# Eight first keys of a product-key layer computed densely instead of gathered, and a first layer put in another order

## The chip, the cores and the metric

The kernel runs on one core of a Trainium2 chip. Its engines work beside one another, each through its own queue in order: TensorE (PE, with its weight loads as PEld), VectorE (DVE), ScalarE (ACT), GpSimd (POOL), and SyncE (SP), which here only issues transfers. The metric is the device time of one execution in microseconds, the median over executions.

## The reference, cut to what matters

A model of 256 tokens and width 1024 in float32: `first_block` has two layers (sliding-window attention beside an S5 state space model, then stick-breaking attention, each with a feed-forward layer), and `second_block` has one (mLSTM beside dilated attention, then PEER). The change concerns the S5 part of the first layer and PEER, the last part of all:

```python
def peer(h, w_query, sub_keys1, sub_keys2, expert_u, expert_v):
    # T = 256 tokens, 8 heads, 128 keys in each of two sets, 128*128 experts of 1024
    s1, s2 = scores of the query halves against sub_keys1, sub_keys2
    v1, i1 = top_k(s1, 16); v2, i2 = top_k(s2, 16)
    vc, ic = top_k(v1[..., :, None] + v2[..., None, :], 16)     # per token and head
    e1 = take(i1, ic // 16); e2 = take(i2, ic % 16)
    idx = e1 * 128 + e2                                          # 128 experts per token
    gate = softmax(vc)
    pre = einsum('td,tkd->tk', x, expert_u[idx])
    a = gelu(pre) * gate
    return einsum('tk,tkd->td', a, expert_v[idx])
```

A token thus uses 128 experts: 16 for each of 8 heads. `e1` is the first key and `e2` the second; an expert's row number is `128 * e1 + e2`. The "second product" is the sum over `expert_v`.

## The kernel before

Most of the kernel is float32 matmul with the weights streamed from memory in tiles of 128 x 1024 (512 KB). A `Stream` loads a raw tile through SP (`fetch`), then `load` makes two float32r halves of it, `whi` by an ACT copy and `wlo` by a DVE subtraction (line 73 is the helper of all DVE and POOL products and sums, line 70 of all ACT copies, L67 of other ACT functions). The tiles live in a ring: 4 `raw`, 3 `whi`, 3 `wlo`, and 4 more of 512 KB under the tag `x2`.

**First layer** (to about 112 us). Its input weights are multiplied while DVE builds the tables of the S5 part: `outer` (L627) forms the products of powers of the state's eigenvalues with the input and output matrices, 128 x 1024 each: two tables `bcd` for the input, and two halves of `clr` for the output. `clr` is zero-filled from memory by SP; half of each table's partitions and columns is written. Before, the `clr` halves are made on DVE in temporaries (`oqw`, `oq`: two products and a sum each) and copied by ACT into place. POOL builds the rotations `ec`, `es` of the scan by doubling, in a temporary with the tag `cmG`. Constants come late: the three masks pass through a temporary `ctmp`, which shares the tag `cmG`, and are cast to bfloat16 by DVE (the last is `swab`). `norm_heads` turns the head's square sums into the factors `rq`, `heads` applies them, then scores and softmax follow, in turns with the scan of the S5 part (`states`, `scan_ops`, `carried`). In `even_core` the order on PE, DVE, ACT and POOL is the order in which the code is written (`tc.manual_schedule`). SP has its own order: the zero fill of `clr`, then the write of `uP` to memory (`ud`) and its reading back (`u4`), then further weights.

**PEER.** The first product is dense: `u_step(e)` (L1765), 128 times, one first key at a time, multiplies the 128 expert rows of `expert_u` with first key e by all 256 tokens, in three float32r products that leave two sums; ACT copies one half of the sum to `GS[:, e]`, the DVE adds the other to it one step later (`u_join`). GS is thus [128 second keys, 128 first keys, 256 tokens]. The top-k work of DVE and POOL is cut in pieces with an estimate of their time and fed in by `run_bg(0.85)`, 0.85 us a step, until step 120. `top_e1` leaves, for each of the 128 experts of a token (on the partitions) and the token (a column), the first key `pe1`, the row number `pidx` and the gate `pg`.

The second product works on gathered rows, four tokens a step, in 64 steps `s`; steps 0 to 31 serve the first 128 tokens (accumulators `acc[0]`, two halves of 512 columns), 32 to 63 the others (`acc[1]`):

- `gather` (L1798): four instructions of POOL, each an indirect transfer that fetches the 128 rows (4 KB each) of one token's experts into a slot of 512 KB. There are 14 slots: the ring's ten and four of `x2`. The chain of waits allows eight gathers in flight.
- `spread` (L1809): four bfloat16 matmuls put e2 on all partitions, and DVE compares it with the partition number (`pcol`): a one-hot of the second key, in a tile `o2` (3 buffers).
- `extract` (L1822): four float32 matmuls of that one-hot with `GS[:, :, token]` bring the 128 first keys' values of the right second key; DVE picks the one of `pe1` by comparing with `iota` and summing (L90), then the row norm, the Gelu (ACT) and the gate follow; the four weights stand in `w32`.
- `apply` (L1837): for two halves of 512 columns and four tokens a matmul of `w32` with the gathered slot.

In a step the order is `spread(s+2)`, `extract(s+1)`, `apply(s)`, `gather(s+3)`. `store` (L1846) fetches the residual in two halves `xr` (in the tag of `o2`), adds the accumulator and writes the output; `store(0)` is issued at s = 31, `store(1)` at the end.

## Time and profile before

| what | us |
|---|---|
| median of 3 runs | 1536.12 (1535.79 to 1536.47) |
| the profiled execution's own time | 1537.89 |
| its span, from the first instruction to the last | 1536.2 |
| first layer, to about | 112 |
| `u_step` loop, about | 835 to 1197 |
| gather phase, about | 1197 to 1536 |

The profiled execution is 1.77 us above the median; 1.7 us of its time lie around the span. The page divides the span into 40 slices of 38.4 us and gives each engine's busy share in tenths; the table of windows does so for any stretch, the timeline lists single instructions with the idle time ahead of each in brackets and what ended it, and the waits add up those times by what ended them. Durations of PE are modelled at their ends, so distances between starts are the surer measure there.

### The profile page before, as it was taken

How to read it: one execution, taken by the hardware profiler on the slowest of the kernel's cores; microseconds unless marked ns; L12 is line 12 of the kernel's file. 1: busy time of each engine (PE TensorE's matmuls, PEld its weight loads, DVE VectorE, ACT ScalarE, POOL GpSimd, SP SyncE). 2: the span in 40 equal slices, each digit the busy share in tenths (PEclk: the TensorE clock that was granted, in tenths of full speed). 3: DMA queues.
4: the chain of work that ended last, by engine and by line, in shares of the span. 5: the costliest groups of instructions: out<-in, count | busy, mean ns of one | idle time of the engine just before them, and what ended most of it. 6: DMA issues, size and time to landing. Idle time of an engine off the chain costs nothing.

```text
span 1536.2 us, 23739 instructions
## 1 busy us (share of the span) xinstructions
PE 1474.2 (96%) x8634; PEld 1126.9 (73%) x8634; DVE 1059.9 (69%) x2519; ACT 668.0 (43%) x1248; POOL 391.7 (26%) x516
## 2 busy tenths in 40 slices
PE   6689999999999999999999999999999999999998
PEld 5568788878988888887888888888888544444443
DVE  7887877675566676776569888999555555555554
ACT  5356555565775555647755445444444000000000
POOL 1820100010100000031110002404000777677764
PEclk9889999999999999999999999999999999999999
DMA  8514655554345555453354555555555999999998
GB/s 319 153 37 164 218 190 191 184 176 138 111 137 185 187 191 189 165 187 123 115 187 161 191 184 179 192 181 191 190 182 184 354 409 408 403 408 409 408 391 333
DMA packets 97389, 341.98 MB, mean 223 GB/s; under 512 B 12016, under 2 KB 15220, under 8 KB 96376
## 3 DMA queue, kind: packets, MB, share of 16 engines
q1 hardware_dynamic: 60120, 206.18, 39.2%
q0 software_dynamic: 36864, 134.23, 22.2%
q8 instruction: 68, 1.11, 0.3%
q14 instruction: 49, 0.40, 0.1%
q10 hardware_dynamic: 288, 0.05, 0.0%
HBM read 337.80 MB, written 2.62 MB: 222 GB/s over the span
## 4 chain that ended last, share of the span: by engine, by line
PE 69%; DMA 16%; DVE 6%; issue 4%; POOL 3%; ACT 2%; SPq 0%; POOLq 0%; DVEq 0%; ACTq 0%
PE mm L375 27%; PE mm L376 14%; DMA vt<-in_ev_dram,pidx 12%; PE acc L385 4%; PE acc L386 4%; PE acc L384 4%; PE mm L367 3%; DMA vx<-in_ev_dram,pidx 3%; PE acc L1843 2%; PE acc L247 1%; DVE wlo L73 1%; POOL vt L1804 1%; PE mm L384 1%; PE mm L385 1%; PE mm L386 1%
## 5 line engine op out<-in xcount | busy, mean ns | idle before, releaser
L375 PE MATMUL mm<-x,whi 128*128 128x512 f32 x1808 | 641.8, 399 | 0.0
L73 DVE TENSOR_TENSOR wlo<-raw,whi 128x1024 fp32r<-128x1024 f32 x345 | 434.2, 1260 | 207.6 <-ACT whi L70 194.9
L376 PE MATMUL mm<-x,wlo 128*128 128x256 f32 x1808 | 507.4, 281 | 2.0 <-DVE wlo L73 2.0
L70 ACT ACTIVATE whi<-raw 128x1024 fp32r<-128x1024 f32 x347 | 366.2, 1057 | 186.6 <-issue 92.0
L375 PEld LDWEIGHTS mm<-x,whi 128*128 128x128 f32 x1808 | 340.4, 188 | 82.5
L376 PEld LDWEIGHTS mm<-x,wlo 128*128 128x128 f32 x1808 | 341.8, 189 | 4.5 <-DVE wlo L73 2.8
L1804 POOL DMA_INDIRECT vt<-in_ev_dram,pidx x184 | 172.5, 938 | 187.1 <-DVE wlo L73 117.0
L1843 PE MATMUL acc<-vt,w 128*32 128x512 f32 x736 | 157.9, 603 | 9.0 <-DMA vt<-in_ev_dram,pidx 4.7
L67 ACT ACTIVATE pk<-pk 128x4 f32<-128x4 f32 x64 | 13.2, 205 | 314.2 <-DVE pk L73 314.2
L70 ACT ACTIVATE gs<-mm 128x256 f32<-128x256 f32 x142 | 54.6, 384 | 207.5 <-PE mm L376 207.5
L90 DVE SCALAR_TENSOR_TENSOR jk<-c,pe,mm 128x128 f32<-128x128 f32 x256 | 89.0, 348 | 72.3 <-PE mm L1826 65.4
L1826 PE MATMUL mm<-gs,o 128*128 128x128 f32 x512 | 124.6, 398 | 1.2 <-DVE o L86 1.2
L73 POOL TENSOR_TENSOR nv<-nss 128x2 f32<-128x2 f32 x5 | 1.0, 195 | 434.3 <-ACT nsq L67 434.3
L1826 PEld LDWEIGHTS mm<-gs,o 128*128 128x128 f32 x512 | 98.2, 202 | 6.2 <-issue 2.2
L1843 PEld LDWEIGHTS acc<-vt,w 128*32 128x32 f32 x736 | 27.7, 108 | 97.4 <-DMA vt<-in_ev_dram,pidx 52.6
L86 DVE TENSOR_SCALAR o<-mm,pcol 128x512 f32<-128x512 f32 x64 | 47.9, 750 | 52.0 <-PE mm L1815 52.0
L1843 PE MATMUL acc<-vx,w 128*32 128x512 f32 x288 | 71.6, 603 | 2.9 <-DMA vx<-in_ev_dram,pidx 1.3
L1804 POOL DMA_INDIRECT vx<-in_ev_dram,pidx x72 | 67.6, 938 | 23.4 <-issue 15.5
L385 PE MATMUL acc<-whi,fhl 128*128 128x512 f32 x176 | 69.9, 397 | 1.4 <-DVE fhl L73 1.4
L384 PE MATMUL acc<-whi,fhh 128*128 128x512 f32 x176 | 69.7, 400 | 1.1 <-ACT fhh L70 1.1
L386 PE MATMUL acc<-wlo,fhh 128*128 128x512 f32 x176 | 69.7, 396 | 0.0
L73 DVE TENSOR_TENSOR gs<-gs,mm 128x256 f32<-128x256 f32 x142 | 58.7, 413 | 10.8 <-ACT gs L70 10.7
(520 smaller groups left out, 2014.4 us busy)
## 6 DMA issues: line engine op xcount, KB each, us to landing
raw<-in_w_dram SPq DMA_DIRECT2D x232, 512.0 KB, 4.3
raw<-in_eu_dram SPq DMA_DIRECT2D x128, 512.0 KB, 3.2
vt<-in_ev_dram,pidx POOLq DMA_INDIRECT x184, 9.5
bcd<-in_cst_dram SPq DMA_DIRECT2D x2, 1024.0 KB, 12.5
u<-in_cst_dram SPq DMA_DIRECT2D x1, 2048.0 KB
clr<-in_cst_dram SPq DMA_DIRECT2D x2, 1024.0 KB, 6.2
vx<-in_ev_dram,pidx POOLq DMA_INDIRECT x72, 9.5
x<-in_x_dram SPq DMA_DIRECT2D x2, 512.0 KB, 4.7
```

Source lines behind the costliest of these rows:

```text
L70: return A.activation(o, i, AF.Copy)
L73: return (e or V).tensor_tensor(o, a, b, op=op)
L86: return (e or V).tensor_scalar(o, a, s1, None, op0=op0)
L90: return V.scalar_tensor_tensor(o, a, s, b, op0=op0, op1=op1, **k)
L375: T.matmul(p, hi[:, ks], x2[:, k].rearrange("p a t -> p (a t)"), start=k == 0, stop=False, skip_group_check=True)
L376: T.matmul(p[:, 0:256], lo[:, ks], xh[:, k], start=False, stop=k == 7, skip_group_check=True)
L384: T.matmul(p, xhi, hi, start=first, stop=False)
L385: T.matmul(p, xlo, hi, start=False, stop=False)
L386: T.matmul(p, xhi, lo, start=False, stop=last)
L1804: G.indirect_dma_start(v, None, evr, bass.IndirectOffsetOnAxis(ap=pidx[:, tok(s, g):tok(s, g) + 1], axis=0))
L1826: T.matmul(p[:, g * 128:(g + 1) * 128], o[:, g * 128:(g + 1) * 128], GS[:, :, tok(s, g)], start=g == 0, stop=True, skip_group_check=True)
L1843: T.matmul(acc[j][hf][32 * g:32 * g + 32], w32[:, g], vs[g][:, hf * 512:(hf + 1) * 512], start=i == 0, stop=i == 31, skip_group_check=True)
```

## The change

**The dense keys.** `ND = 8` first keys, 120 to 127, leave the gathers: each gather now carries a bounds check at row 128 * 120 - 1 and is told to leave out rows beyond it without an error; `extract` compares with 120 keys instead of 128, so such experts get the weight 0. What they add to the output is computed for all 256 tokens: `gate_in` and `gate_out` form, for eight tokens a step in steps 0 to 31, the gate of each (second key, dense first key) by a bfloat16 product of one-hots (the gate itself split in three bfloat16 parts `gp`), and multiply it with the Gelu of GS; `dense(i)`, at s = 32, 36, ... 60, multiplies that [128 second keys, 256 tokens] matrix by the 512 KB of `expert_v` for first key 120 + i. `dense_in` splits both into float32r halves and starts the next load. The accumulators are zeroed by four matmuls, since products of two kinds now go into them.

**What goes with it.** GS is stored as [8, 256 tokens, 16], so that the eight dense keys and each token's keys lie together: `u_step`'s copy and add write 64 bytes apart. The gathers have 10 fixed slots (raw 2, whi 2, wlo 2, x2 4), the other four ring tiles serve the dense part. The order in a step is `apply(s)`, `gather(4)`, `spread(s+3)`, `extract(s+2)`, then the gates or the dense product. `o2` has 2 buffers. `store(0)` is issued at s = 60, after `dense(7)`. `spread(0)` and `spread(1)` move into the `u_step` loop.

**The first layer.** The zero fill of `clr` moves behind the reading of `ud`, two weight fetches ahead of its write; `ctmp` takes the tag `qT`; the second `bcd` table waits for a weight split; `clr[:, 0]` is built on DVE inside the heads' code without ACT's copy, `clr[:, 1]` on POOL; the last product of `norm_heads` moves to POOL; the first scan's steps 4 and 5 come after the second softmax.

```diff
-        tmp = sb.tile([128, 4, 512], F32, name="ctmp", tag="cmG")
+        tmp = sb.tile([128, 2, 512], F32, name="ctmp", tag="qT")
...
+        for _ in range(2):
+            W.fetch()
         S.dma_start(ud.rearrange("(m q) t -> q m t", m=4), uP.rearrange("q m t c -> q m (t c)"))
...
+        outer(bcd[0:1], 0, ((pr, bbr, pi, bbi, OP.subtract),), (0,), V)
+        with tc.issue_after(W.los[9].ins):
+            outer(bcd[1:2], 0, ((pr, bbi, pi, bbr, OP.add),), (2,), V)
+        def clr0():
...
+            mul(b_[:, 0], bj(pr), bm(c_re))
+            mul(b_[:, 1], bj(pi), bm(cneg))
+            yield
+            for h in range(2):
+                hs = slice(h * 64, (h + 1) * 64)
+                add(clr[hs, 0, :, :, h, :], b_[hs, 0], b_[hs, 1])
+            yield
...
+        clr1 = lambda: outer([clr[:, 1]], 1, ((pr, cneg, pi, c_re, OP.subtract),), None, G)
...
-        rq3 = norm_heads(rq, ssv, ssq, r, 20, sb, V)
+        rq3 = norm_heads(rq, ssv, ssq, r, 20, sb, V, G)
         taps()
+        clr1()
...
-    GS = p2.tile([128, 128, 256], F32, name="gs")
+    GS = p2.tile([128, 8, 256, 16], F32, name="gs")
...
-        cp(GS[:, e], p[:, 256:512])
-        halves.append((GS[:, e], p))
+        cp(GS[:, e // 16, :, e % 16], p[:, 256:512])
+        halves.append((GS[:, e // 16, :, e % 16], p))
...
+                G.indirect_dma_start(v, None, evr, bass.IndirectOffsetOnAxis(ap=pidx[:, t:t + 1], axis=0), bounds_check=128 * (128 - ND) - 1, oob_is_err=False)
...
-        o = p2.tile([128, 512], F32, name="o2", tag="o2", bufs=3)
+        o = p2.tile([128, 512], F32, name="o2", tag="o2", bufs=2)
...
-            stt(jk, iota, pe1[:, t:t + 1], p[:, g * 128:(g + 1) * 128], OP.is_equal, OP.mult, accum_out=pk[:, g:g + 1])
+            stt(jk[:, 0:128 - ND], iota[:, 0:128 - ND], pe1[:, t:t + 1], p[:, g * 128:g * 128 + 128 - ND], OP.is_equal, OP.mult, accum_out=pk[:, g:g + 1])
...
-            xr = p2.tile([128, 512], F32, name="xr", tag="o2", bufs=3)
+            xr = p2.tile([128, 512], F32, name="xr", tag="o2", bufs=2)
...
+    def gate_in(n, o):
...
+        for i in range(8):
+            act(o[:, i], iota, AF.Abs, bias=pe2n[:, 8 * n + i:8 * n + i + 1])
+        act(o, o, AF.Relu, bias=1.0, scale=-1.0)
+        a = p2.tile([128, 8, 4, ND], BF16, name="ga", tag="cand", bufs=2)
+        tt(a[:, :, 3], iota[:, None, 128 - ND:128].to_broadcast([128, 8, ND]), pe1[:, t8, None].to_broadcast([128, 8, ND]), OP.is_equal)
+        mul(a[:, :, 0:3], a[:, :, 3:4].to_broadcast([128, 8, 3, ND]), gp[:, t8, :, None].to_broadcast([128, 8, 3, ND]))
...
+        act(d, d, AF.Gelu)
...
+    def gate_out(n, o):
...
+        for i in range(8):
+            T.matmul(p[:, i * 3 * ND:(i + 1) * 3 * ND], o[:, i], a[:, i, 0:3].rearrange("p k e -> p (k e)"), start=True, stop=True,
+                     skip_group_check=True)
+        V.tensor_reduce(jk[:, 0:8 * ND], p[:, 0:24 * ND].rearrange("p (t k e) -> p t e k", t=8, k=3), axis=AX.X, op=OP.add)
+        d = GS[:, 7, 8 * n:8 * n + 8, 16 - ND:16]
+        mul(d, d, jk[:, 0:8 * ND].rearrange("p (t e) -> p t e", t=8))
...
+    def dense(i, hi, lo):
...
+                for l, r in ((ah, hi), (al, hi), (ah, lo)):
+                    T.matmul(acc[j][hf], l[:, sl], r[:, c], start=False, stop=False, skip_group_check=True)
...
+        gather(10)
+        S.dma_start(raw_, ev[128 - ND])
+        extract(0)
+        spread(2)
+        extract(1)
+        gate_in(0, o_[:, 0])
         for s in range(NS):
...
+            apply(s)
+            gather(4)
+            if s + 3 < NS:
+                spread(s + 3)
             if s + 2 < NS:
...
+                extract(s + 2)
+            if s < 32:
+                if s < 31:
+                    gate_in(s + 1, o_[:, (s + 1) % 2])
+                gate_out(s, o_[:, s % 2])
+                if s == 31:
+                    dense_in(0, raw_, hi_, lo_)
+            elif s % 4 == 0:
+                i = s // 4 - 8
+                dense(i, hi_, lo_)
+                if i + 1 < ND:
+                    dense_in(i + 1, raw_, hi_, lo_)
+                else:
+                    store(0)
         store(1)
```

**Three places in the order of instructions.** A row is a line of the kernel, the operation, output and inputs by their names, the shape, and a count where rows of one form follow one another; names in brackets are the queues and engines that a row waits for (DMAHW are SP's transfers). The first is SP at the kernel's end, before:

```order
L118 DMA raw<-in_eu_dram 128x1024 [waits DMAHW4_49,DVE_49]
L1850 DMA xr<-xd 128x512 [waits DVE_49,PE_49] x2
L1852 DMA out_dram<-xr 128x512 [waits DVE_49] x2
L1850 DMA xr<-xd 128x512 [waits DMAHW5_49,DVE_49,PE_49]
L1850 DMA xr<-xd 128x512 [waits DMAHW3_49,DMAHW6_49,DVE_49,PE_49]
L1852 DMA out_dram<-xr 128x512 [waits DMAHW7_49,DVE_49]
L1852 DMA out_dram<-xr 128x512 [waits DMAHW0_49,DVE_49]
```

After:

```order
L1921 DMA vraw<-in_ev_dram 128x1024 [waits DMAHW7_49,DMAHW0_49,DVE_49]
L1884 DMA xr<-xd 128x512 [waits DVE_49,PE_49]
L1886 DMA out_dram<-xr 128x512 [waits DVE_49]
L1884 DMA xr<-xd 128x512 [waits DMAHW2_49]
L1884 DMA xr<-xd 128x512 [waits PE_49]
L1886 DMA out_dram<-xr 128x512 [waits DVE_49]
L1884 DMA xr<-xd 128x512 [waits DMAHW5_49]
L1886 DMA out_dram<-xr 128x512 [waits DVE_49]
L1886 DMA out_dram<-xr 128x512 [waits DMAHW0_49,DVE_49]
```

The two loads of `store(0)` stood side by side; now the second stands behind the first half's output and waits for a transfer of SP, and a load of `store(1)` likewise.

The second is DVE at the end, with the multiply-sums of `extract` (L90), its three products and the add of `xr`. Before:

```order
L86 TENSOR_SCALAR o_14506<-mm,pcol 128x512
L90 SCALAR_TENSOR_TENSOR jk,pk<-c_75,pe_8104,mm 128x128 x4
L73 TENSOR_TENSOR pk<-pk,rb_p 128x4
L73 TENSOR_TENSOR pk<-pk,pg 128x4
L73 TENSOR_TENSOR w_14521<-pk,eye 128x128
L90 SCALAR_TENSOR_TENSOR jk,pk<-c_75,pe_8104,mm 128x128 x4
L73 TENSOR_TENSOR pk<-pk,rb_p 128x4
L73 TENSOR_TENSOR pk<-pk,pg 128x4
L73 TENSOR_TENSOR w_14544<-pk,eye 128x128
L73 TENSOR_TENSOR xr<-xr,acc 128x512 x2
```

After:

```order
L73 TENSOR_TENSOR w_15757<-pk,eye 128x128
L86 TENSOR_SCALAR o_15784<-mm,pcol 128x512
L90 SCALAR_TENSOR_TENSOR jk,pk<-c_75,pe_8100,mm 128x120 x4
L73 TENSOR_TENSOR pk<-pk,rb_p 128x4
L73 TENSOR_TENSOR pk<-pk,pg 128x4
L73 TENSOR_TENSOR w_15799<-pk,eye 128x128
L73 TENSOR_TENSOR xr<-xr,acc 128x512 x2
L90 SCALAR_TENSOR_TENSOR jk,pk<-c_75,pe_8100,mm 128x120 x4
L73 TENSOR_TENSOR pk<-pk,rb_p 128x4
L73 TENSOR_TENSOR pk<-pk,pg 128x4
L73 TENSOR_TENSOR w_15848<-pk,eye 128x128
L73 TENSOR_TENSOR xr<-xr,acc 128x512 x2
```

The two adds of `store(0)` stand ahead of the last four multiply-sums now.

The third is the first layer: DVE from the tables `oqw`, `oq` (temporaries of `clr`) and the split `wlo` to the head norm (`ssq`, `ssv`), before:

```order
L73 TENSOR_TENSOR oqw<-pr,ppb 128x1024
L73 TENSOR_TENSOR bcd_95<-oq_719,oq_720 64x64x16 x2
L73 TENSOR_TENSOR oqw<-pi,cneg 128x1024
L73 TENSOR_TENSOR wlo<-raw,whi 128x1024 x2
L73 TENSOR_TENSOR oqw<-oqw 128x1024
L73 TENSOR_TENSOR oq_732<-pr,cneg 128x1024
L73 TENSOR_TENSOR oq_733<-pi,ppb 128x1024
L73 TENSOR_TENSOR oq_732<-oq_732,oq_733 128x1024
L73 TENSOR_TENSOR wlo<-raw,whi 128x1024
L703 TENSOR_REDUCE ssq<-sk__789 128x2
L703 TENSOR_REDUCE ssq<-sk__792 128x2
L73 TENSOR_TENSOR r_819<-nr 128x2
```

After:

```order
L73 TENSOR_TENSOR wlo<-raw,whi 128x1024 x2
L73 TENSOR_TENSOR oq_719<-pr,bbt 128x1024
L73 TENSOR_TENSOR oq_720<-pi,bbt 128x1024
L73 TENSOR_TENSOR bcd_95<-oq_719,oq_720 64x64x16 x2
L73 TENSOR_TENSOR wlo<-raw,whi 128x1024
L715 TENSOR_REDUCE ssq<-sk__775 128x2
L715 TENSOR_REDUCE ssq<-sk__778 128x2
L73 TENSOR_TENSOR r_805<-nr 128x2
L73 TENSOR_TENSOR ssv<-ssq,r_805 128x20
L87 TENSOR_SCALAR ssv<-ssv 128x20
```

And POOL there, after, from the end of its rotations `ec`, `es`:

```order
L73 TENSOR_TENSOR ec<-cmG 128x16x32
L73 TENSOR_TENSOR es<-cmG 128x16x32
L73 TENSOR_TENSOR rq<-rq,nr 128x20
L73 TENSOR_TENSOR cmG<-pr,cneg 128x1024
L73 TENSOR_TENSOR cmG<-pi,ppb 128x1024
L73 TENSOR_TENSOR clr<-cmG 64x64x16 x2
L73 TENSOR_TENSOR sc<-sc,rd 128x8x128
```

The six operations of `clr` are gone from DVE ahead of the norm; `rq` and four operations of `clr` have come to POOL behind the rotations.

## Rows read from the trace of the kernel before

**Rows 1.** The page, 40 slices: busy share of the DMA engines in tenths

```profile
DMA  8514655554345555453354555555555999999998
```

**Rows 2.** Table of windows, gather phase: busy us (instructions) by engine, clock, DMA, GB/s

```profile
core 0: us, PE busy (x) PEld busy (x) DVE busy (x) ACT busy (x) POOL busy (x), PEclk, DMA share, GB/s
1250.00:1300.00 50.00, 48.77 (x276) 21.34 (x275) 27.33 (x120) 2.05 (x10) 36.66 (x40) 1.00 1.03 409
```

**Rows 3.** Timeline of PE, gather phase: start us, duration us, engine, line, operation

```profile
1204.14 0.40 PE L1815 MATMUL mm<-e2b,idb 128*128 128x128 bf16 x4
1204.38 1.94 PE L1826 MATMUL mm<-gs,o 128*128 128x128 f32 x8
1206.25 1.92 PE L1843 MATMUL acc<-vt,w 128*32 128x512 f32 x16
1208.11 0.40 PE L1815 MATMUL mm<-e2b,idb 128*128 128x128 bf16 x4
...
1304.56 0.40 PE L1815 MATMUL mm<-e2b,idb 128*128 128x128 bf16 x4
1309.68 0.40 PE L1815 MATMUL mm<-e2b,idb 128*128 128x128 bf16 x4
```

**Rows 4.** Waits, 1200 to 1537 us: engine, line, released by: us, times, longest

```profile
PEld acc L1843 <- DMA vt<-in_ev_dram,pidx: 52.6, 52, 2.0
```

**Rows 5.** Timeline of POOL, gather phase: early, and steady

```profile
1207.40 0.94 POOL L1804 DMA_INDIRECT vt<-in_ev_dram,pidx  x1 [0.30 <-issue]
...
1302.18 0.94 POOL L1804 DMA_INDIRECT vt<-in_ev_dram,pidx  x1 [0.34 <-issue]
```

**Rows 6.** Groups by line, 960 to 1075 us: count, busy us, mean ns

```profile
L70 ACT ACTIVATE whi<-raw 128x1024 fp32r<-128x1024 f32 x41 | 43.2, 1054 | 0.0
L70 ACT ACTIVATE gs<-mm 128x256 f32<-128x256 f32 x41 | 15.8, 385 | 61.2 <-PE mm L376 61.2
L73 DVE TENSOR_TENSOR gs<-gs,mm 128x256 f32<-128x256 f32 x42 | 17.2, 409 | 0.0
L67 ACT ACTIVATE gs<-gs 128x128 f32<-128x128 f32 x1 | 0.3, 310 | 0.0
```

**Rows 7.** Table of windows, `u_step` loop, columns as in rows 2

```profile
870.00:900.00 30.00, 30.00 (x171) 26.03 (x170) 26.34 (x90) 14.68 (x22) 0.00 (x0) 1.00 0.53 181
960.00:990.00 30.00, 30.00 (x173) 26.06 (x173) 29.79 (x53) 14.25 (x22) 13.66 (x13) 1.00 0.57 193
```

**Rows 8.** The page, DMA issues: count, median us from issue to landing

```profile
vt<-in_ev_dram,pidx POOLq DMA_INDIRECT x184, 9.5
```

**Rows 9.** The tile `xr`, its four loads and four adds

```profile
DMA to landing us min/median/max: 2.0/6.2/6.9
```

**Rows 10.** Timeline, end of the kernel

```profile
1530.16 1.90 PE L1843 MATMUL acc<-vt,w 128*32 128x512 f32 x10 [0.22 <-DMA vt<-in_ev_dram,pidx]
1531.24 0.69 DVE L73 TENSOR_TENSOR xr<-xr,acc 128x512 f32<-128x512 f32 x1 [5.56 <-PE acc L1843]
```

**Rows 11.** Groups by line and shape, 1200 to 1537 us

```profile
L90 DVE SCALAR_TENSOR_TENSOR jk<-c,pe,mm 128x128 f32<-128x128 f32 x256 | 89.0, 348 | 72.3 <-PE mm L1826 65.4
```

**Rows 12.** Groups by line and shape on DVE, 112 to 180 us

```profile
L73 DVE TENSOR_TENSOR os<-yg,sg 128x256 f32<-128x256 f32 x4 | 2.5, 623 | 0.4 <-ACT sg L67 0.4
L73 DVE TENSOR_TENSOR sol<-os,soh 128x256 fp32r<-128x256 f32 x4 | 1.7, 425 | 2.0 <-ACT soh L70 2.0
```

**Rows 13.** Timeline of POOL, first layer

```profile
39.20 2.97 POOL L73 TENSOR_TENSOR cmG<-ec,zr 128x16 f32<-128x16 f32 x1 [10.92 <-DVE swab L188]
...
71.47 1.26 POOL L73 TENSOR_TENSOR es<-cmG 128x512 f32<-128x512 f32 x1
```

**Rows 14.** Timeline of DVE, first layer

```profile
31.70 0.16 DVE L73 TENSOR_TENSOR zr<-t,t 128x16 f32<-128x16 f32 x1
...
63.54 1.33 DVE L73 TENSOR_TENSOR wlo<-raw,whi 128x1024 fp32r<-128x1024 f32 x1 [3.27 <-ACT whi L70]
...
66.24 1.07 DVE L73 TENSOR_TENSOR ssv<-ssq,r 128x20 f32<-128x20 f32 x1
...
74.93 0.69 DVE L73 TENSOR_TENSOR qn<-acc,rq 128x512 f32<-128x512 f32 x1
```

More of the change, by code (lines that the diff above doesn't have):

```diff
@@ L466, in even_layer @@
         mul(kn_g, qn_g, kn_g)
-        for i in range(2):
-            zeros(clr[:, i].rearrange("p s j h q -> p (s j h q)"))
         a_re, a_im = ppa[:, 0:16], ppa[:, 16:32]
@@ L585, in even_layer @@
                                            uds[:, :, 0:256 - 64 * d_])
+        for i in range(2):
+            zeros(clr[:, i].rearrange("p s j h q -> p (s j h q)"))
         b_re, b_im, c_re, c_im = (ppb[:, i * 256:(i + 1) * 256].rearrange("p (s q) -> p s q", s=16) for i in range(4))
@@ L924, in even_core @@
         smax(0, 0)
+        next(clr0)
         scores(1, 0)
@@ L1781, in tile_kernel @@
     NS = 64
+    ND = 8
     slots = []
```

131 lines of the change are left out of this document (77 added, 54 removed).

## The prediction

> **What bounds the kernel now.** I read the page first: of a 1536.2 us span the last eighth is the only stretch in which the DMA digits stand at 9 [rows 1]. That stretch is the end of PEER, the 64 steps in which expert rows are gathered and applied, and the table of windows says what bounds it: from 1250 to 1300 us the DMA engines are busy all the time at 409 GB/s, while DVE works 27 of 50 us [rows 2]. A step gathers 4 x 128 rows of 4 KB, 2.10 MB, which at 409 GB/s takes 5.13 us; PE's steps are 5.12 us apart (1304.56 to 1309.68), while at the phase's start, with gathers in hand, they were 3.97 us apart (1204.14 to 1208.11: 0.24 of `spread`, 1.87 of `extract`, 1.86 of `apply`) [rows 3]. The waits agree: the weight loads of `apply` wait 52.6 us for gathered rows in `vt` slots alone [rows 4]. POOL, which issues the gathers, is close behind: one instruction takes 0.94 us plus 0.30 us of issue where nothing holds it, 1.24 us, and 1.28 us in the steady stretch [rows 5]. Four are 4.97 us. So a step whose DMA work shrinks gains at most 5.12 - 4.97 = 0.15 us, 10 us over 64 steps, before POOL is late instead. That cap decides much below.
>
> Ahead of it, the `u_step` loop (128 steps of some 2.8 us) is bound by PE with DVE just behind it, and the first layer (20 to 112 us) by a chain through DVE, POOL and ACT. The change touches all three.
>
> **Gathers, first half (s < 32).** Of the 32768 gathered rows 2356 name a first key of 120 or more, as I counted from the reference's inputs: 1100 in the first 128 tokens, 1256 in the others. If the bounds check drops them, DMA in this half falls 6.7%, to 4.79 us a step, and POOL's 4.97 us rules. But new work enters the same steps. On ACT `gate_in` adds eight 128x128 Abs (a 128x128 activation takes 310 ns), a Relu of 128x1024 (nearest 1054 ns) [rows 6] and a small Gelu: some 3.8 us. It starts behind the Gelu of `extract`, which comes some 5.0 us after the step's start (1.86 + 0.24 + 1.87 on PE, then 1.0 of DVE: the last multiply-sums and a product). PE's `gate_out`, one step later and 3.97 us into it, waits for it; so the step cannot be under 5.0 + 3.8 - 3.97 = 4.8 to 5.0 us. PE itself has 3.97 plus eight small bfloat16 matmuls (four with 128 columns take 0.24 us at the head of a step, so 0.5 to 0.8 us): it is covered. Three engines within 0.2 us of one another seldom give the largest alone: I take 5.06 us, **-2 us** in 32 steps; bounds -5 (POOL's floor) and +6 (a step of 5.3 us).
>
> **Gathers, second half.** Seven of the eight dense loads of 512 KB start at s = 31 to 52: 3.67 MB at 409 GB/s are +9.0 us of DMA. The dropped rows are 1256 x 4 KB = 5.14 MB, -12.6 us if all sixteen engines lose alike, and nothing if the busiest keeps its rows. No row of before shows which engine takes which row, but the eight heads, whose sixteen rows each lie together in a gather, drop between 2.0% and 12.6%, so an even loss is unlikely. I take a third, -4: **+5 us**. The bounds are -4 (POOL's cap of 0.15 us x 32, whatever DMA saves) and +9 (nothing dropped, or a dropped row that costs a packet). PE has 3.97 + 2.8 / 4 = 4.7 us a step here (a 512-column matmul is 0.23 us by the `u_step` rows: 173 matmuls of mean 384 columns in 30 us, [rows 7]), which DMA covers.
>
> The Trainium skill, page "DMA: Bandwidth & Descriptors", section "The descriptor swizzle", ties a row's engine to its partition in a 128-partition transfer. By that rule my count of the inputs leaves the busiest engine 1995 of its 2048 rows, 2.6%, and the second half's saving is -4.3 us as an estimate, in place of the -12.6 of an even loss. No row of before shows it, and the rule speaks against the change.
>
> `store(0)` leaves s = 31, where its two reads and two writes of 256 KB (1.05 MB) shared the queue: **-2.6 us**. Ten slots in place of fourteen matter little: a gather lands 9.5 us after its issue [rows 8], 7.4 gathers deep, but when the fourth of a step lands only six can be in flight until `apply` has read them. With the zeroing matmuls, `extract(1)` and `gate_in(0)` ahead of the first `apply`, **+2 us** (0 to +4).
>
> **The end.** Here the change adds a wait that I think it pays in full. `xr` and the spread's output share tag `o2`, now with 2 buffers. When `store(0)` is issued at s = 60, one of them holds `spread(63)`, so its second `xr` takes the buffer of the first: in SP's order that load waits for the first output's landing. Both adds stand in DVE ahead of the four multiply-sums of `extract(63)`, so `apply(63)` waits for the store. From the start of `apply(60)`: its matmuls, `spread`, `extract(62)` end at 4.0; the first `xr` lands 6.2 us later [rows 9] at 10.2, with gathers still flowing; add 0.69 [rows 10], the output lands at about 16.5; the second `xr`, now alone, lands 2.0 us later [rows 9] at 18.6; add, four multiply-sums of 0.39 (0.348 [rows 11] and the read of the accumulator), the three small products and the Gelu: `w32(63)` at 22. Without it `apply(63)` starts when the last gather lands, at 15.3. **+7 us**, 5 to 10. What follows it is as before (6.0 us from 1530.16 to the span's end [rows 10]).
>
> **The `u_step` loop.** GS becomes [8, 256, 16]: the ACT copy (385 ns) and the DVE add (409 ns) of each step [rows 6] now step 64 bytes from element to element. The nearest strided row, a DVE product that writes 16 bytes apart, takes 623 ns where its contiguous like takes 425 [rows 12]: +0.2 us on 409, up to +0.4 as both a read and the write are strided. From 960 to 990 us DVE is busy 29.79 of 30 us [rows 7], ten steps with no room; most other stretches leave about 3 us in 30, 0.28 us a step. Twenty steps at 0.1 us: **+2 us**; 0, if DVE's slack takes all, to +8 (0.2 us in forty steps). The new gate splits in `top_e1` are fourteen small operations, taken into this. `extract` reads GS contiguously now, which may shorten its 1.87 us; PE waits for DMA there, so I count nothing.
>
> The Trainium skill, page "SBUF — State Buffer", section on the port swizzle, note on SBUF cachelines, says that accesses that each go to a new 16-byte line pay a penalty. The rows of the 623 ns product agree, and for 64 bytes it would speak for the upper end, +8 us.
>
> **First layer.** Before, POOL's rotation chain waits 10.92 us for the last mask cast (`swab`) until 39.20 and ends at 72.73 [rows 13]; on DVE six operations for `clr`, and on ACT four copies, stand ahead of `whi`, for which DVE waits 3.27 us; then the head norm runs from 66.24 until `qn` starts at 74.93 [rows 14], its first operations on 20 columns at 1.07 us beside POOL. After, the table's work is behind the heads, POOL's buffer no longer waits for `swab` but for the angles that DVE has by 31.86 [rows 14], some 7 us earlier, and the norm's last product is queued on POOL behind the chain, at about 66: the heads start some 8.5 us earlier. But four 128x1024 operations (1.33 us [rows 14]) come back on DVE ahead of the scans, and four on POOL run beside the heads' DVE work and slow it as the 1.07 us operations were slowed. The fetches moved ahead of `ud` find their weights earlier and change no wait on the chain. **-4 us**, -9 to +1.
>
> **Sum.** -2 + 5 - 2.6 + 2 + 7 + 2 - 4 = +7.4 us on the profiled execution's 1537.89 us. That one is 1.8 us above the median of 1536.12, so in medians 1543.5: I say 1543 us.
>
> **Rivals.** *The gathers run at POOL's pace (faster).* Skipped rows thin all engines, every step is near 4.97 to 5.0 us (-9), the store leaves (-2.6), the first layer gives -7, the end costs 5 and `u_step` 1: -12, some 1524 us; with half of the first layer's gain 1529. For it: the 0.04 us by which POOL is throttled, and DMA's busy share of 1.03. Against it: the heads' uneven shares and the dense loads. Chance 0.31.
> *Gains and the end cancel.* The first layer gives -8 and the rest +8: within 0.2%, which is about what a measurement of this kernel can tell from no change, 1536 us. Chance 0.15.
> *The checked gather is slower (slower, another mechanism).* If the bounds check lengthens POOL's instruction, it decides from 0.04 us on, since 1.24 + 0.04 = 1.28 is DMA's pace; at +0.1 us the loss is 256 x 0.06 = 15 us on top of the rest, 1558 us. The same time results if dropped rows still take their packet and the strided writes cost their upper end: +4 and +6 more. Against it: before has no checked gather, so nothing supports a price. Chance 0.16.
> *The forecast*, 1538 to 1550: chance 0.38.
>
> Slower by over 0.2% are the last two, less a little: 0.52; faster 0.32; same 0.16. The range must reach into the faster case and the slower gather: 1525 to 1558.
>
> **What would show it.** Right: gathers of POOL still 0.94 us; fewer bytes on their queue; PE's steps at 5.0 to 5.1 us in the first half and 5.2 to 5.3 in the second; two adds of `xr` on DVE ahead of the last multiply-sums, 7 us apart, with PE idle; the add of `u_step` at 0.6 us or more; heads from about 67 us. Wrong: steps of 5.0 us throughout; an `apply(63)` that starts with its last gather; or a POOL instruction over 1.0 us.

## The result, and the profile after

| | before | after |
|---|---|---|
| median of four runs, us | 1535.95 (1534.87 to 1536.47) | 1556.55 (1553.96 to 1557.53) |
| the profile's span, us | 1536.2 | 1555.7 |

The change makes the kernel slower: the ratio of the times is 1.013, with an interval of 1.0118 to 1.0143, 20.6 us. The forecast was 7 us slower, so the sign was right and the size a third of what came.

From the page of the kernel after: the span; the granted clock, DMA's busy share and its rate in 40 slices (38.9 us each here); and the gathers' queue.

```profile
span 1555.7 us, 25283 instructions
PEclk9889999999999999999999999999999999999998
DMA  8515655543335555543444554555556999999997
GB/s 324 143 42 180 216 189 187 185 165 130 137 115 200 187 190 189 184 151 115 151 176 164 189 185 170 182 183 191 196 184 208 333 375 374 376 386 381 383 362 278
...
q0 software_dynamic: 36864, 124.60, 21.3%
```

The same queue before:

```profile
q0 software_dynamic: 36864, 134.23, 22.2%
```

Against [rows 1] and [rows 2] the last eighth still has 9s for DMA, but the rate has gone from 409 to about 380 GB/s. The queue has moved 124.60 MB where it was 134.23: the rows are indeed left out, some 2355 by the bytes where the prediction counted 2356. It still has 36864 packets. The table of windows shows the same, and which engines have more to do now (ACT 35.76 of 50 us where it had 2.05):

```profile
core 0: us, PE busy (x) PEld busy (x) DVE busy (x) ACT busy (x) POOL busy (x), PEclk, DMA share, GB/s
1250.00:1300.00 50.00, 40.94 (x352) 19.45 (x352) 37.20 (x167) 35.76 (x105) 37.94 (x39) 0.97 1.00 377
1400.00:1450.00 50.00, 47.51 (x299) 21.82 (x299) 29.90 (x117) 6.65 (x15) 36.68 (x36) 1.00 1.01 382
```

Where the time went is read most safely from the starts of single matmuls, at the same places of the program. Before, in order: the last matmul of the `u_step` loop, and the first of `apply(4)`, `apply(32)` and `apply(60)`.

```profile
1195.78 0.28 PE L376 MATMUL mm<-x,wlo 128*128 128x256 f32 x1
...
1218.73 1.06 PE L1843 MATMUL acc<-vt,w 128*32 128x512 f32 x6
...
1364.39 1.18 PE L1843 MATMUL acc<-vt,w 128*32 128x512 f32 x5
...
1512.32 1.06 PE L1843 MATMUL acc<-vt,w 128*32 128x512 f32 x6
```

After:

```profile
1196.90 0.28 PE L376 MATMUL mm<-x,wlo 128*128 128x256 f32 x1
...
1224.38 1.06 PE L1877 MATMUL acc<-vx,w 128*32 128x512 f32 x6
...
1371.42 0.62 PE L1877 MATMUL acc<-vx,w 128*32 128x512 f32 x2
...
1523.85 1.05 PE L1877 MATMUL acc<-vraw,w 128*32 128x512 f32 x4
```

| stretch | before, us | after, us | difference |
|---|---|---|---|
| to the last matmul of the `u_step` loop | 1195.8 | 1196.9 | +1.1 |
| from there to `apply(4)` | 23.0 | 27.5 | +4.5 |
| `apply(4)` to `apply(32)` | 145.7 | 147.0 | +1.4 |
| `apply(32)` to `apply(60)` | 147.9 | 152.4 | +4.5 |
| `apply(60)` to the end of the span | 23.9 | 31.8 | +7.9 |

The sum is +19.4 of the 19.5 us between the spans. No single stretch holds the loss. These are one profile against one: where two kernels run the same code up to the end of the `u_step` loop, as after and the last but one of the experiments do, two profiles still differ by 1.2 us there.

**POOL.** Two gathers of the steady stretch, to be held against [rows 5]:

```profile
1297.16 0.99 POOL L1836 DMA_INDIRECT vx<-in_ev_dram,pidx  x1 [0.30 <-issue]
1298.45 0.99 POOL L1836 DMA_INDIRECT vx<-in_ev_dram,pidx  x1 [0.30 <-PE mm L1910]
```

An instruction takes 0.99 us where it took 0.94, and the next starts after the same 0.30 us of issue, 1.29 us apart in all. POOL waits for nothing here beyond its issue: the idle time is 0.30 us again, not the 0.34 of the steady row in [rows 5], although DMA's share is still 1.00. From `gather` 16 to 128, the rows of `apply(4)` to `apply(31)`, it takes 146.2 us with 1.0 us of idle time beyond the issue, and those applies take 147.0: in the first half POOL has become the engine that sets the step. Four such gathers are 5.17 us; before, DMA set 5.12.

**The end.** The timeline from the first residual load of `store(0)`:

```profile
1529.01 0.33 SPq L1884 DMA_DIRECT2D xr<-xd  x1
...
1535.54 0.69 DVE L73 TENSOR_TENSOR xr<-xr,acc 128x512 f32<-128x512 f32 x1 [4.05 <-DMA xr<-xd]
1536.26 0.34 SPq L1886 DMA_DIRECT2D out_dram<-xr  x1
...
1542.39 0.80 SPq L1884 DMA_DIRECT2D xr<-xd  x2
1545.12 0.69 DVE L73 TENSOR_TENSOR xr<-xr,acc 128x512 f32<-128x512 f32 x1 [8.89 <-DMA xr<-xd]
...
1547.88 0.29 DVE L73 TENSOR_TENSOR w<-pk,eye 128x128 f32<-128x128 f32 x1
1548.23 1.06 PE L1877 MATMUL acc<-vwhi,w 128*32 128x512 f32 x2 [8.41 <-DVE w L73]
```

It went in the order that the prediction has: first load at 1529.01, add at 1535.54, output, second load only at 1542.39, second add at 1545.12, and behind it on DVE `w32(63)`; PE waited 8.41 us for it. `apply(63)` starts 24.4 us after `apply(60)` (1548.23 - 1523.85).

**The start of the gather phase** (ACT's `gate_in(0)`, PE's `extract(2)`, and the next gather):

```profile
1204.56 2.43 ACT L67 ACTIVATE vraw<-c,pe2n 128x128 bf16<-128x128 f32 x8
...
1207.98 0.24 ACT L67 ACTIVATE gs<-gs 128x64 f32<-128x64 f32 x1
1208.27 1.16 PE L1857 MATMUL mm<-gs,o 128*128 128x128 f32 x8 [3.82 <-ACT gs L67]
...
1213.37 0.98 POOL L1836 DMA_INDIRECT vwlo<-in_ev_dram,pidx  x1 [4.08 <-PE acc L1877]
```

`extract(2)` waits 3.82 us for the Gelu of `gate_in(0)`, which overwrites the dense columns of the tokens 0 to 7 in GS; token 2 is one that `extract(2)` reads. `apply(1)` is late by that, and POOL, with ten slots, stands 4.08 us until it has read them.

**The clock of PE** falls at both places. Windows of the kernel after, and one of before, with the columns as above:

```profile
1204.50:1208.20 3.70, 0.00 (x0) 0.00 (x0) 1.75 (x6) 3.67 (x11) 2.89 (x3) 1.00 0.94 338
1209.80:1213.00 3.20, 3.20 (x16) 0.43 (x8) 2.68 (x16) 1.80 (x7) 0.00 (x0) 0.50 0.91 321
1548.20:1551.00 2.80, 2.77 (x16) 0.59 (x16) 0.69 (x1) 0.00 (x0) 0.00 (x0) 0.50 0.27 94
```

```profile
1200.00:1520.00 320.00, 308.97 (x1730) 139.28 (x1730) 176.01 (x757) 12.94 (x63) 230.41 (x246) 1.00 1.02 404
```

After PE has stood still from 1204.50 to 1208.20, `apply(1)` runs at 0.50, the lower of the clock's two levels (1.2 of 2.4 GHz), and takes 3.5 us to the next matmul (1209.55 to 1213.07), where `apply(2)` takes 1.9. The gather that POOL waits for is released at its end. `apply(63)`, after the wait of 8.41 us, runs at 0.50 too. Before, the clock is 1.00 throughout. So some 1.7 us of the loss at the start, and some 1.3 at the end (the matmuls of `apply(63)` on one slot start 0.86 us apart, those of `apply(2)` 0.44), come from the clock that fell with the wait; this is read from the trace, and no run isolates it.

**The first layer.** DVE from the head's factors to the first scan, after:

```profile
67.30 0.69 DVE L73 TENSOR_TENSOR qn<-acc,rq 128x512 f32<-128x512 f32 x1 [0.33 <-POOL rq L73]
...
76.06 1.22 DVE L73 TENSOR_TENSOR clq<-pr,ppb 128x1024 f32<-128x1024 f32 x1
77.20 1.22 DVE L73 TENSOR_TENSOR clq<-pi,cneg 128x1024 f32<-128x1024 f32 x1
...
79.93 2.45 DVE L73 TENSOR_TENSOR clr<-clq 64x1024 f32<-64x1024 f32 x2
...
83.88 1.22 DVE L872 TENSOR_TENSOR_SCAN g<-rho_t,g 128x512 f32<-128x512 f32 x1
```

And that scan before:

```profile
85.66 1.17 DVE L860 TENSOR_TENSOR_SCAN g<-rho_t,g 128x512 f32<-128x512 f32 x1
```

The heads start at 67.30 instead of 74.93 [rows 14], 7.6 us earlier; the scan at 83.88 instead of 85.66, 1.8 us earlier.

**The `u_step` loop**, ACT's copy and DVE's add of GS from 960 to 1075 us, and a window:

```profile
L70 ACT ACTIVATE gs<-mm 128x256 f32<-128x256 f32 x41 | 25.9, 631 | 55.6 <-PE mm L376 55.6
L73 DVE TENSOR_TENSOR gs<-gs,mm 128x256 f32<-128x256 f32 x41 | 25.5, 621 | 0.0
```

```profile
960.00:990.00 30.00, 29.79 (x169) 25.40 (x168) 29.79 (x50) 15.81 (x22) 13.67 (x13) 1.00 0.50 182
```

The copy has gone from 385 to 631 ns and the add from 409 to 621 ns [rows 6]; PE, which was busy for all 30 us from 960 to 990, has lost 0.21 there [rows 7].

### The profile page after: what moved, and what is told of

Same layout as the page of the kernel before. It is cut to its first block, busy times and chain, and to the rows that moved or that the text cites. A ratio compares the mean times of both kernels' runs of the same rounds, so it can differ in the third digit from the quotient of the medians.

```text
span 1555.7 us, 25283 instructions
## 1 busy us (share of the span) xinstructions
PE 1461.0 (94%) x8989; PEld 1119.9 (72%) x8990; DVE 1132.7 (73%) x2704; ACT 811.0 (52%) x1580; POOL 420.3 (27%) x521
## 3 DMA queue, kind: packets, MB, share of 16 engines
q0 software_dynamic: 36864, 124.60, 21.3%
## 4 chain that ended last, share of the span: by engine, by line
PE 65%; DVE 11%; DMA 10%; issue 5%; POOL 4%; ACT 4%; POOLq 0%; SPq 0%; DVEq 0%; ACTq 0%
PE mm L375 23%; PE mm L376 12%; PE acc L385 4%; PE acc L386 4%; PE acc L384 4%; PE acc L1877 4%; DMA vx<-in_ev_dram,pidx 3%; PE mm L367 3%; DVE wlo L73 3%; DMA vwhi<-in_ev_dram,pidx 2%; DMA vraw<-in_ev_dram,pidx 2%; ACT vraw L67 2%; PE mm L1857 2%; PE acc L247 1%; POOL cmG L73 1%
## 5 line engine op out<-in xcount | busy, mean ns | idle before, releaser
L70 ACT ACTIVATE gs<-mm 128x256 f32<-128x256 f32 x142 | 86.9, 612 | 188.7 <-PE mm L376 188.7
L1836 POOL DMA_INDIRECT vx<-in_ev_dram,pidx x100 | 100.8, 1008 | 33.5 <-issue 19.5
L90 DVE SCALAR_TENSOR_TENSOR jk<-c,pe,mm 128x120 f32<-128x120 f32 x256 | 86.8, 339 | 25.3 <-PE mm L1910 9.2
L1877 PE MATMUL acc<-vx,w 128*32 128x512 f32 x400 | 97.7, 610 | 3.7 <-DMA vx<-in_ev_dram,pidx 3.5
L73 DVE TENSOR_TENSOR gs<-gs,mm 128x256 f32<-128x256 f32 x142 | 85.7, 603 | 10.8 <-ACT gs L70 10.8
L1836 POOL DMA_INDIRECT vraw<-in_ev_dram,pidx x52 | 53.0, 1019 | 129.6 <-DVE wlo L73 110.7
L1857 PE MATMUL mm<-gs,o 128*128 128x128 f32 x512 | 72.8, 283 | 8.2 <-ACT gs L67 7.6
L67 ACT ACTIVATE vraw<-c,pe2n 128x128 bf16<-128x128 f32 x256 | 77.8, 386 | 0.0
L1877 PE MATMUL acc<-vwhi,w 128*32 128x512 f32 x208 | 65.3, 644 | 12.0 <-DVE w L73 8.4
L1857 PEld LDWEIGHTS mm<-gs,o 128*128 128x128 f32 x512 | 62.8, 192 | 10.9 <-ACT gs L67 8.5
```

What stands on the lines that cost most here:

```text
L67: return A.activation(o, i, f, **k)
L70: return A.activation(o, i, AF.Copy)
L73: return (e or V).tensor_tensor(o, a, b, op=op)
L90: return V.scalar_tensor_tensor(o, a, s, b, op0=op0, op1=op1, **k)
L1836: G.indirect_dma_start(v, None, evr, bass.IndirectOffsetOnAxis(ap=pidx[:, t:t + 1], axis=0), bounds_check=128 * (128 - ND) - 1, oob_is_err ...
L1857: T.matmul(p[:, g * 128:(g + 1) * 128], o[:, g * 128:(g + 1) * 128], GS[:, :, tok(s, g)], start=g == 0, stop=True, skip_group_check=True)
```

## The experiments

All kernels but the last two were run on chips where the kernel before takes 1576 to 1582 us, those two (both repairs without the check, and what is worth keeping) on one where it takes 1536 as it does for the result. Each kernel is compared with before on its own chip.

**What the parts cost.** The first layer's part alone (all hunks of the diff ahead of the line 700 of before, and that of `even_core`), expected:

> The kernel before with the first-layer part of the change alone. Theory 1 (the first layer gains little: the two traces are 1.8 us apart from the end of that layer on, where I had forecast 4): 1.8 us faster than before, 1534.2, with every stretch from 120 us on 1.5 to 1.8 us early. Rival (the part gains the 4 us forecast and the rest of the change takes some of it back in the first layer): 1532.

Measured: ratio 0.9987 (0.9973 to 1.0002), 2 us faster by its middle. The interval reaches 1, and it holds the sizes of both theories. The trace speaks for theory 1: its heads start at 67.54 and its first scan at 84.14, 1.5 us earlier than before's.

The kernel before with a bounds check that drops nothing:

```diff
-            G.indirect_dma_start(v, None, evr, bass.IndirectOffsetOnAxis(ap=pidx[:, tok(s, g):tok(s, g) + 1], axis=0))
+            G.indirect_dma_start(v, None, evr, bass.IndirectOffsetOnAxis(ap=pidx[:, tok(s, g):tok(s, g) + 1], axis=0), bounds_check=128 * 128 - 1, oob_is_err=False)
```

> The kernel before with a bounds check on every gather, at the table's last row, so that no row is dropped. Theory 1 (the check itself lengthens POOL's instruction, as it stands at 0.99 us after the change where it was 0.94): gathers 0.99 us, 1.29 us apart instead of 1.28, steps of 5.17 us instead of 5.12, 3 us slower in all, 1539. Rival (the length comes from the dropped rows, or from ACT and DVE beside POOL): gathers 0.94 us, steps 5.12, no change.

Measured: ratio 0.9995 (0.9983 to 1.0007). Its POOL row of the gather phase, from the table of groups:

```profile
L1804 POOL DMA_INDIRECT vt<-in_ev_dram,pidx x175 | 173.7, 992 | 84.2 <-issue 40.5 <-remote 22.8 <-PE mm L1826 10.1
```

The instruction's 992 ns stand against 938 [rows 5: 0.94], with no row dropped and no gate work beside it: the price is the check's own. The time didn't move: on this chip the steps are 5.9 us (165.4 us from `apply(4)` to `apply(32)`), so something else held them, and this run can't tell what the price does where POOL is the bound. A second run of the same kernel, on another chip:

> The kernel before with a bounds check on every gather at the table's last row, so that nothing is dropped. Theory 1: the check alone makes POOL's instruction 0.99 us, gathers 1.29 us apart; where the kernel before has steps of 5.12 us set by DMA, they become 5.17, 3 us slower in all. Rival (no price of its own, or POOL not the later one): no change.

Measured: 1.0005 (0.9994 to 1.0017). The price in POOL's row is shown; what it costs where steps are 5.12 us was not measured by this kernel.

The kernel after without the check (`bounds_check=..., oob_is_err=False` taken out), so that all rows come and the dense keys' rows get the weight 0. It ran on three chips:

> The kernel after without the bounds check: all rows are fetched again, those of the dense keys get the weight 0. Theory 1 (POOL's checked gather at 1.29 us apart sets the steps after the change, so the 9.6 MB that are dropped buy nothing): POOL falls to 1.24, DMA becomes the bound again at 5.13 us a step and 9 us of dense loads: within 4 us of after, 1553 to 1558. Rival (DMA still sets the steps after the change): the 9.6 MB come back at 409 GB/s, 23 us slower than after, 1580.

> The kernel after without the bounds check: all rows are fetched, those of the dense keys get the weight 0. Theory 1 (POOL's checked gather, 1.29 us apart, sets the steps after the change, so that the 9.6 MB dropped buy little): within 4 us of after. Rival (DMA still sets the steps): the 9.6 MB come back at the chip's rate, over 20 us slower than after.

> The kernel after without the bounds check, all rows fetched, those of the dense keys with the weight 0. Theory 1 (POOL sets the steps after the change): within 4 us of after. Rival (DMA sets them): over 20 us slower than after.

Measured: 1.0119 (1.0092 to 1.0146), 1.0125 (1.0100 to 1.0150) and 1.0120 (1.0098 to 1.0142), where the kernel after itself, run on the second of these chips alone, had

> The kernel after, unchanged, beside the next three on one chip. Where gathers move at about 405 GB/s in the kernel before, 20 us slower than before; the yardstick for the three. If memory is slower on the chip and before itself takes longer, both theories expect the gap to before to shrink or hold, since DMA and not POOL then sets the steps of both.

1.0136 (1.0108 to 1.0163). Dropping 9.63 MB, 23.5 us of transfer at 409 GB/s, buys nothing that these runs can see, so the rival, 20 us slower, doesn't hold on these chips. It doesn't follow that POOL sets the steps there: they are some 5.9 to 6.0 us, well above POOL's 5.17 with the check and 4.97 without, and the runs with half the bytes below show that on such chips neither bound holds them.

**The waits at the end and at the start.** `store(0)` in the raw tile of the dense part, free by then:

```diff
-    def store(j):
+    def store(j, into=None):
...
-            xr = p2.tile([128, 512], F32, name="xr", tag="o2", bufs=2)
+            xr = into[:, c] if into is not None else p2.tile([128, 512], F32, name="xr", tag="o2", bufs=2)
...
-                    store(0)
+                    store(0, raw_)
```

> The kernel after with the two residual halves of store(0) in the free raw tile of the dense part, so that neither load waits for an output or for the spread's buffer. Theory 1 (the wait at the end costs 7 us, as forecast): apply(63) starts with its last gather, 6 to 8 us faster than after, 1549. Rival (the last gathers, which POOL issues late, set the end anyway): 0 to 2 us faster, 1555.

> The kernel after with the two residual halves of store(0) in the dense part's free raw tile, so that no load waits for an output or for the spread's buffer. Theory 1: apply(63) starts with its last gather, 6 to 8 us faster than after. Rival (the last gathers set the end): 0 to 2 us faster.

Measured: 1.0101 (1.0065 to 1.0138) and 1.0128 (1.0095 to 1.0162), against 1.0136 for after on the second chip (it was not run on the first): faster in both, but within the intervals, and with steps that differ between two profiles of the same chip by more than this. The timelines decide the mechanism. After, on the second chip, with its two adds and `apply(63)`:

```profile
1583.99 0.69 DVE L73 TENSOR_TENSOR xr<-xr,acc 128x512 f32<-128x512 f32 x1 [3.73 <-DMA xr<-xd]
...
1591.45 0.69 DVE L73 TENSOR_TENSOR xr<-xr,acc 128x512 f32<-128x512 f32 x1 [6.78 <-DMA xr<-xd]
...
1594.56 0.13 PEld L1877 LDWEIGHTS acc<-vwhi,w 128*32 128x32 f32 x2 [11.91 <-DVE w L73]
```

And with the repair, where both adds stand together and the next thing that PE waits for is a gather:

```profile
1584.37 1.28 DVE L73 TENSOR_TENSOR vraw<-vraw,acc 128x512 f32<-128x512 f32 x2
...
1588.58 0.14 PEld L1877 LDWEIGHTS acc<-vraw,w 128*32 128x32 f32 x2 [0.85 <-DMA vraw<-in_ev_dram,pidx]
```

From `apply(60)` to the end of the span the two profiles have 33.8 and 23.5 us. So the wait is the one named, and it goes. The medians alone leave its size open.

The groups of `gate_in` in another order, tokens 128 to 255 first:

```diff
+    GO = list(range(16, 32)) + [4 * b + a for a in range(4) for b in range(4)]
...
-        t8 = slice(8 * n, 8 * n + 8)
+        m_ = GO[n]
+        t8 = slice(8 * m_, 8 * m_ + 8)
```

> The kernel after with the groups of eight tokens that gate_in takes in turn put in another order (tokens 128 to 255 first), so that no product of extract reads columns of GS that a Gelu has just overwritten. Theory 1 (the 3.8 us wait of extract(2) for gate_in(0) at the phase's start, which holds POOL back by 4.1 us, and four shorter ones cost what they show): 4 to 6 us faster than after. Rival (POOL catches up, or ACT's gate work of some 4 us a step holds PE just as long one matmul later): 0 to 1 us.

Measured: 1.0188 (1.0146 to 1.0230), no faster, rather slower. `extract(2)` no longer waits, but `gate_out(0)` behind it waits 4.52 us for ACT instead, and POOL still stands 4.09 us at that place. Both repairs together:

> The kernel after with both repairs: the residual halves of store(0) in the dense part's free raw tile, and gate_in's groups of eight tokens in the order that keeps its Gelu away from what extract reads. Theory 1 (start and end cost 4 and 7 us, the rest is POOL at 1.29 us a gather): 10 us faster than after, still 10 us slower than before, with POOL idle for nothing but its issue from the first apply on. Rival (the gate work or the dense loads hold the steps, and both repairs only move the wait): under 5 us faster than after.

Measured: 1.0090 (1.0069 to 1.0111), 7 us less than the 1.0136 that after had on another chip, with intervals that just touch; between the two theories.

**Without the dense work.** `gate_in`, `gate_out`, `dense_in`, `dense` and the first dense load taken out; the dense keys are missing from the output:

> The kernel after without gate_in, gate_out, the dense loads and the dense products; what the eight dense keys add to the output is left out. Theory 1 (POOL's checked gather is the floor of a step): steps of 5.17 us in both halves, the start without its 4 us wait, the end's wait of 7 us as it was: 10 us faster than after. Rival (the rows dropped let DMA go faster than before once the dense work is away): steps of 4.8 to 5.0 us, 20 us faster than after or more.

Measured: 1.0061 (1.0044 to 1.0078), 12 us less than after had on another chip. It is still slower than before, although it has 7% fewer bytes in the gather phase and none of the dense work. The rest of the change is left in it: the check, the ten slots, the wait at the end, the stride of GS and the first layer. The theory's 10 us were met, its steps of 5.17 us not: they are 5.9 us on this chip.

**Half the bytes.** On those chips DMA moves about 360 GB/s in the gather phase, and to take DMA out of the way the gathers fetch 2 KB a row, from another place of the table:

```diff
-            G.indirect_dma_start(v, None, evr, ...
+            G.indirect_dma_start(v[:, 0:512], None, evh, ...
...
-                T.matmul(acc[j][hf][32 * g:32 * g + 32], w32[:, g], vs[g][:, hf * 512:(hf + 1) * 512],
+                T.matmul(acc[j][hf][32 * g:32 * g + 32], w32[:, g], vs[g][:, 0:512],
```

> The kernel before with gathers of 2 KB instead of 4 KB a row (from another place of the table, the product on the first half for both halves; the output is another): DMA has 2.6 us of work in a step. Both theories: POOL's unchecked gathers, 1.24 us apart, set steps of 4.97 us, some 16 us faster than before. This is POOL's floor without the check.

> The same with a bounds check that drops nothing. Theory 1 (the check alone costs POOL 0.05 us an instruction): gathers 1.29 us apart, steps of 5.17 us, 12 us slower than without it. Rival (POOL's wider spacing after the change came from something else): as without it.

> The kernel after with gathers of 2 KB, the products on the first half. Theory 1 (POOL's checked gather is the floor of the steps after the change): 5.17 us a step in both halves, hardly faster than after, with the start's and the end's waits as they were. Rival A (the gate work on ACT, DVE and PE sets the first half): first half at 5.24 us or more as after, second half shorter. Rival B (DMA sets the steps after): both halves go to 5.0 us or less, 20 us faster.

> The same without the check: DMA and POOL's check are both out of the way. Theory 1: steps of 4.97 us in both halves, 12 us faster than with it. Rival A (gate work): the first half stays at 5.1 us or more. This tells what the gate work would allow had the check been free.

Measured: 1.0004 (0.9987 to 1.0021), 0.9988 (0.9972 to 1.0003), 1.0103 (1.0057 to 1.0150) and 1.0107 (1.0078 to 1.0136). The gains that the theories put on half the bytes failed: they change nothing. The check changes nothing either, as its rival has it, though not for the rival's reason: POOL's instruction is 1.00 us with it and 0.95 without here too. The windows of the first:

```profile
1250.00:1300.00 50.00, 40.21 (x250) 20.37 (x240) 21.72 (x95) 1.64 (x8) 32.15 (x34) 0.83 0.63 180
1259.00:1264.00 5.00, 2.56 (x13) 0.59 (x16) 4.14 (x22) 0.41 (x2) 3.79 (x4) 0.50 0.49 129
1267.00:1272.00 5.00, 5.00 (x38) 2.42 (x40) 2.05 (x11) 0.20 (x1) 3.78 (x5) 1.00 0.70 205
```

DMA is busy 63% of the time and moves 180 GB/s, POOL is busy 32 of 50 us; neither holds the steps, which are 6.0 us. The granted clock of PE is 0.83 here, where it was 1.00 in the gather phase of [rows 2]: it goes between its two levels, as from 1259 to 1264 us (0.50) and from 1267 to 1272 (1.00), again and again in this phase on that chip. Why it does so there and not on the other is open. So these runs say nothing on POOL's floor; they say that on such a chip the gather phase isn't bound by what the change saves either.

**Both repairs and no check**, on a chip like that of the result:

> The kernel after with both repairs (start and end) and without the bounds check, all rows fetched. Theory 1 (the dropped bytes buy nothing, since POOL with the check is no faster than DMA without it): as g_fix within 4 us, some 10 us faster than after. Rival (DMA sets the steps after the change): 20 us slower than g_fix.

Measured: 1554.04 us, ratio 1.0117 (1.0100 to 1.0133), against 1.0130 for after: 2 us faster than after, not the 10 expected, and nowhere near the 20 us slower of the rival. Two windows and two lines of its start:

```profile
1250.00:1300.00 50.00, 45.32 (x354) 19.84 (x346) 37.19 (x162) 36.65 (x107) 36.04 (x39) 1.00 1.03 408
1400.00:1450.00 50.00, 47.43 (x294) 20.64 (x293) 29.50 (x114) 6.58 (x15) 33.20 (x36) 1.00 1.02 408
```

```profile
1206.89 0.39 PE L1912 MATMUL mm<-ga,vraw 128*128 128x24 bf16 x8 [2.73 <-ACT vraw L67]
...
1210.66 0.94 POOL L1836 DMA_INDIRECT vwlo<-in_ev_dram,pidx  x1 [2.86 <-PE acc L1877]
```

With POOL's unchecked 0.94 us, DMA is back at 408 GB/s and 1.02 to 1.03 of its time: it sets the steps again, with all rows and the dense loads. By the stretches of the table above (one profile against one, spans 1551.4 and 1555.7): to the loop's end -1.2, to `apply(4)` -1.5, 28 steps of the first half +1.8 (148.8 us), 28 of the second +1.7 (154.1), from `apply(60)` to the end -5.0 (26.8). So dropping the rows, check and all, is worth 3.5 us of the 23.5 that their bytes take, by the starts of the applies; by the starts of the 224 gathers that serve these steps it is 1.5 us (301.7 and 300.2). Both are as small as the difference of two profiles, and the kernel with both repairs and the check was not run on this chip. The end is shorter by 5 us, and the start by 1.5: `extract(2)` doesn't wait any more, but `gate_out(0)`, the next on PE, waits 2.73 us for the same ACT work, `apply(1)` again runs at the clock's lower level (0.50 from 1206.6 to 1209.6), and POOL still stands 2.86 us. The wait that only moves is the rival that I had set against that repair.

**What is worth keeping.** The kernel before with the first layer's part, and `store(0)` behind the last gather:

```diff
-            if s == 31:
+            if s == 62:
                 store(0)
```

and `o2`, `xr` with 4 buffers.

> The kernel before with the first-layer part of the change, and store(0) issued after the last gather (s = 62) with 4 buffers of the tag o2, so that its 1 MB no longer shares the queue with the gathers. Theory 1 (first layer 1.8 us, store(0) 2.6 us at s = 31 of which 1 us comes back at the end): 3 us faster than before. Rival (the store's transfers cost the same wherever they lie, the first layer's gain is lost by the gather phase): no change.

Measured: 1533.58 us against 1536.25, ratio 0.9982 (0.9972 to 0.9992): faster than before by the 3 us expected, and so than after. The two steps beside the old place of `store(0)` take 10.2 us (1354.27 to 1364.51 for `apply(31)` to `apply(33)`) where they took 11.6. The prediction put 2.6 us on the store.

## Why the prediction was right in sign and wrong in size

| term | forecast, us | measured, us |
|---|---|---|
| first layer | -4 | -1.6 at the start of the `u_step` loop |
| `u_step` loop | +2 | +2.0 by 1111 us, +0.7 more at its end |
| start and slots | +2 | +4.5 |
| gathers, first half | -2 | +1.4 |
| gathers, second half, with `store(0)` gone | +5 - 2.6 | +4.5 |
| end | +7 | +7.9 |

**Right.** The end: mechanism and place, and the size within 1 us. Part of the last is luck: the second add, put 18.6 us after `apply(60)`, started 21.3 us after, and `apply(63)`, put at 22, at 24.4; but the last gather that `apply(63)` needs before, put at 15.3, came at 17.8, so that the errors cancel. What follows was to be as before, 6.0 us, and took 7.4 at the lower clock. The `u_step` loop: +0.2 us on each of the two operations, and +2.0 us where DVE has no slack. The rows are dropped, and `extract` is faster (its matmuls 283 ns where they were 398), which the prediction counted as nothing.

**The step that failed most: POOL's floor.** The prediction took 4.97 us for four gathers as the cap on what a step can gain. With the check it is 5.17, above the 5.12 that DMA needed before. It had named this as a rival, with the right point from which it decides ("from 0.04 us on"), gave it 0.16 and no price, since before has no checked gather. The check costs 0.054 us, just over that point. From then on no dropped row can shorten a step, so the -2 of the first half and the -4 of saved rows in the second were not to be had; the first half came 3.4 us above its term, and +1.4 is 28 steps of the 0.05 us between 5.17 and 5.12. The price need only exceed 0.04. It explains the lost gains, not the whole error: of the 12 us by which the stretches came out above their terms, the gathers hold 5.5, the start 2.5, the first layer 2.4, the end and the `u_step` loop 1.6.

The groups of the gather phase show ACT's Abs of `gate_in` after the change:

```profile
L67 ACT ACTIVATE vraw<-c,pe2n 128x128 bf16<-128x128 f32 x256 | 77.8, 386 | 0.0
```

**The second half** has a floor of 28 x 5.17 = 144.8 us by POOL and took 152.4. Two of POOL's rows there tell where the rest lies:

```profile
1373.81 2.00 POOL L1836 DMA_INDIRECT vx<-in_ev_dram,pidx  x1 [0.30 <-PE acc L1877]
...
1404.09 0.99 POOL L1836 DMA_INDIRECT vx<-in_ev_dram,pidx  x1 [1.69 <-PE acc L1877]
```

A dense product stands between two applies on PE, so the slots of the next come free late and POOL stands (1.69 us at 1404.09); and three gathers that begin beside DVE's 1.23 us split of the dense tile take 1.9 to 2.0 us instead of 0.99. In all, POOL's 112 gathers for these steps take 154.0 us, with 6.1 us of idle time beyond the issue and 3.3 us of longer instructions. An engine that sets the pace can't make such time up. The prediction had put the dense loads on DMA alone and spread the dense product evenly over four steps of PE, where DMA would cover it. That these waits make up the 7.6 us above the floor is read from the trace, and no run isolates it. One idle stretch of 1.80 us, before the gather at 1487.26, has no releaser in the trace.

**The start** was put at +2 for the work ahead of the first `apply`, and that cost nothing: `apply(0)` starts 5.3 us after the loop, where it started 6.5 after it. The +4.5 come behind it, from the wait of `extract` for `gate_in` through GS, which was not seen, and from the clock that falls after it, which no term of the prediction has. Undoing the wait gave 1.5 us, since `gate_out` waits for the same ACT work (Abs takes 386 ns, not the 310 of [rows 6]).

**The first layer**: the heads are 7.6 us earlier, 8.5 were forecast. But `clq` and `clr` (2.4 and 2.5 us) stand between the heads and the first scan, and all of it is on the path, with 0.8 us more on each of two products of the heads that run beside POOL. The forecast took 4.5 of the 8.5 us back for this; up to the scan 5.8 of the 7.6 went.

**The range**, 1525 to 1558, held the result at its edge, and that is luck: its upper end is the rival of the checked gather at +0.1 us an instruction, 15 us. At the measured price the same sum gives 256 x 0.014 = 3.6 us (1.294 against DMA's 1.28). The error was in how the terms fell: all six came out worse than put, two of them for one cause. Two smaller slips bear on nothing: the cap of 0.15 us x 32 is 4.8 us, not 4, and the rival at POOL's pace with half of the first layer's gain comes to some 1527 us, not 1529.
